# All 512 first-part tokens by row in a decoder trunk: 1024 row steps, 544 dense tokens, and more row steps with each product of the second part

## The chip, the core and the metric

The kernel runs on one core of a Trainium2 chip. The metric is device time in microseconds (us), the median of several executions. The profile shows one execution of the same program, with its engines: TensorE (PE, its weight loads shown apart as PEld), VectorE (DVE), ScalarE (ACT), GpSimd (POOL) and the queue engine SyncE (SP), and the 16 DMA engines.

## What is computed

One decoder layer for 1024 prompt tokens and 32 sample tokens, all in fp32, with model width 1024. The cut of the reference that matters here is the expert layer (PEER) at the end:

```
qh = x @ w_q                              # 8 heads x 256
v1, i1 = top_k(qh[..., :128] @ keys_1.T, 16);  v2, i2 = top_k(qh[..., 128:] @ keys_2.T, 16)
sc, ci = top_k(v1[:, None] + v2[None, :], 16)      # per token and head: 16 of 16384 experts
e, g   = expert numbers, softmax(sc)
hid    = gelu(einsum('thkd,td->thk', u_tab[e], x))
y      = einsum('thkd->td', (g * hid) * v_tab[e])
out    = LayerNorm2(ALPHA * h + y)
```

Before it stand the input product, a state-space scan with its convolution, a dilated window attention, the output product and LayerNorm1. So each token needs 128 rows of `u_tab` and 128 rows of `v_tab` (1024 floats each), picked by its own expert numbers.

## The kernel before

**Two parts.** The prompt is worked in two parts of 512 tokens (`PARTS`), the 32 sample tokens with the first. Each part runs `first` (queries, keys, values, attention, and the convolutions of B and C), `second` (twelve products for x with convolution and scan, then twelve for the gate z), `third` (the output product, 16 half products called `WO`, and LayerNorm1) and `route` (16 query products and the search for the experts). A product is `step`: a 1024x128 weight against all tokens of the part, in three passes (high x high, high x low, low x high), 24 or 48 matmuls. In the second part the split weights `whi` and `wlo` are read back from memory (`ws`), 2 x 512 KB for each product.

**Two ways through the expert layer.** After part one, its tokens' experts are known. For 448 of its 512 tokens (`TG`) the rows go one by one: generator `gathers` makes row steps. A row step is one indirect DMA on POOL (L1845) that fetches, for 128 tokens, one expert row each (128 x 4 KB, 512 KB), and one DVE operation over 128x1024: for `u` a product with the token and its sum (L1871), for `v` a scaled addition into the accumulator (L1876). A block of 128 tokens takes 128 u steps and 128 v steps; the last block has 64 tokens, laid as two halves over the 128 partitions, and takes 64 and 64. That is 896 steps. Six row buffers (`ROWS`) let row k+5 be fetched behind step k.

All other tokens, the second part's 512, the 32 samples and the last 64 of part one (`EXTRA`), 608 together (`TE`), go the dense way in `dense`: the hidden values of all 16384 experts for all tokens, 256 products of a 1024x128 weight with 48 matmuls each, 320 and 288 columns wide (`TPC`). For this, `gates` first builds a table of gates: for each four tokens DVE makes a one-hot pair `oo` (L1624), POOL weighs one half (L1626), PE multiplies (L1633), ACT stores (L1643). There are 152 such groups: 8 for the samples, 16 for the 64 extra tokens, 128 for the second part. The first six dense products (`EARLY` ticks) run beside this work. The other 250 follow, and each reads a 512 KB weight that ACT and POOL split into `whi` and `wlo` (L366, L367; one split in seven is DVE's), and pieces `g` of the gate table.

**What sets the order.** Code is issued in the order of ticks. A product has a few ticks, spread over its matmuls, and at each tick every open lane runs by its rate. `GATHER` gives the row steps for each product of the four stages of the second part, and the last entry the rate for each tick beside the table; afterwards `dense` spreads what is left evenly over its products. All engines take their instructions in that order, so a row step stands in the queues of POOL and DVE between the instructions of the product. `EARLY` gives 152 ticks in all. At the end, the last two products are cut in two pieces of tokens, and between them the kernel issues all that is left of the row lane.

## Time and profile before

| | us |
|---|---|
| median of 3 runs | 3749.65 (3748.82 to 3754.33) |
| the profiled execution | 3745.24 |
| its span in the trace | 3743.3 |

| engine | busy us | share |
|---|---|---|
| PE | 3461.4 | 92% |
| DVE | 2600.5 | 69% |
| POOL | 2231.0 | 60% |
| ACT | 1205.4 | 32% |

DMA moved 994.91 MB, 266 GB/s over the span. The shares are means over stages with different limits. Part one takes the trace up to some 870 us, the second part up to 1720, the table of gates from 1730 to 2020, and the dense products from there to the end. A busy PE counts pipelined matmuls and is not PE at its peak: the pace of PE is read from the starts of matmuls that follow each other.

### The profile page before, as it was taken

To read this page: it belongs to the slowest core of one execution; us is meant where nothing else is said; L and a number is where in the kernel's file an instruction comes from. 1 tells how busy PE (TensorE), PEld (TensorE's weight loads), DVE (VectorE), ACT (ScalarE), POOL (GpSimd) and SP (SyncE) were. 2 spreads that over 40 slices of the span, in tenths; PEclk is the share of its full clock that TensorE was granted. 3 is DMA by queue.
4 is the path that set the end of the run, shared out by engine and by line. 5 is a ranking of instruction groups with operands and counts; after the bars stand their busy time and mean duration, and the time that the engine had idled before them with its cause. 6 is when DMAs were issued, how large, how long until landed. Compare 5 with 4: busy or idle time off the path is not lost.

```text
span 3743.3 us, 61910 instructions
## 1 busy us (share of the span) xinstructions
PE 3461.4 (92%) x22691; PEld 3132.8 (84%) x22691; DVE 2600.5 (69%) x5394; ACT 1205.4 (32%) x2195; POOL 2231.0 (60%) x2138
## 2 busy tenths in 40 slices
PE   7999999989799888896778999999999999999998
PEld 6757778988567666675777999999999999999997
DVE  2325654379668987589998867677767667777775
ACT  3422224252343233123565222222232222223223
POOL 3303555333444676313887877777778777777774
PEclk9999899999899999997889999999999999999999
DMA  7565447996557669742557999999999999999994
GB/s 248 192 207 185 144 149 241 371 343 214 163 168 293 235 217 337 304 141 72 202 204 267 342 328 339 336 322 314 320 326 356 330 329 335 321 315 321 333 330 138
DMA packets 452624, 994.91 MB, mean 266 GB/s; under 512 B 47712, under 2 KB 158688, under 8 KB 449376
## 3 DMA queue, kind: packets, MB, share of 16 engines
q1 hardware_dynamic: 323296, 521.14, 41.1%
q0 software_dynamic: 129024, 469.82, 34.6%
q8 instruction: 179, 2.93, 0.3%
q14 instruction: 125, 1.02, 0.1%
HBM read 845.18 MB, written 174.34 MB: 272 GB/s over the span
## 4 chain that ended last, share of the span: by engine, by line
PE 53%; DVE 16%; DMA 5%; POOL 5%; issue 4%; ACT 2%; SPq 0%; POOLq 0%; DVEq 0%; ACTq 0%
PE P L447 42%; PE P L1767 5%; DVE oo L1624 2%; DMA wlo<-ws 2%; DVE cv L751 2%; DVE row L1871 1%; PE P L712 1%; POOL row L1845 1%; DVE mr L1363 1%; PE P L689 1%; POOL oo L1626 1%; DVE keys L1367 1%; DVE keys L1361 1%; PE P L1633 1%; POOL eq L1564 1%
## 5 line engine op out<-in xcount | busy, mean ns | idle before, releaser
L367 POOL TENSOR_TENSOR wlo<-wraw,whi 128x512 fp32r<-128x512 f32 x524 | 678.5, 1300 | 495.6 <-ACT whi L366 438.5
L366 ACT ACTIVATE whi<-wraw 128x512 fp32r<-128x512 f32 (+1 forms) x668 | 406.1, 625 | 1305.7 <-PE P L447 563.7
L447 PE MATMUL P<-hh,whi 128*128 128x320 f32 (+3 forms) x2648 | 656.2, 313 | 13.4 <-DMA whi<-ws 5.7
L447 PE MATMUL P<-hl,whi 128*128 128x320 f32 (+3 forms) x2648 | 653.4, 311 | 3.2 <-POOL hl L1318 2.9
L447 PE MATMUL P<-hh,wlo 128*128 128x320 f32 (+3 forms) x2648 | 647.4, 310 | 7.6 <-DMA wlo<-ws 3.9
L1876 DVE SCALAR_TENSOR_TENSOR P<-row,hid,P 128x1024 f32<-128x1024 f32 x448 | 575.8, 1285 | 40.3 <-DMA row<-in_v,ecol 23.9
L1871 DVE SCALAR_TENSOR_TENSOR row<-row,P 128x1024 f32<-128x1024 f32 x403 | 478.8, 1214 | 66.1 <-DMA row<-in_u,ecol 29.6
L1845 POOL DMA_INDIRECT row<-in_u,ecol x384 | 386.9, 1008 | 191.6 <-DVE row L1871 100.9
L447 PEld LDWEIGHTS P<-hh,whi 128*128 128x128 f32 x2648 | 445.5, 191 | 24.9 <-DMA whi<-ws 7.0
L447 PEld LDWEIGHTS P<-hh,wlo 128*128 128x128 f32 x2648 | 443.7, 190 | 17.7 <-DMA wlo<-ws 5.9
L447 PE MATMUL P<-xh,whi 128*128 128x272 f32 (+4 forms) x1288 | 431.2, 345 | 27.0 <-ACT xh L366 15.0
L447 PEld LDWEIGHTS P<-hl,whi 128*128 128x128 f32 x2648 | 444.9, 191 | 12.6 <-POOL hl L1318 4.2
L1845 POOL DMA_INDIRECT row<-in_v,ecol x384 | 375.9, 979 | 118.4 <-DVE P L1876 47.1
L447 PE MATMUL P<-xl,whi 128*128 128x272 f32 (+4 forms) x1288 | 418.8, 335 | 7.4 <-POOL xl L367 6.8
L447 PE MATMUL P<-xh,wlo 128*128 128x272 f32 (+4 forms) x1288 | 417.4, 334 | 3.2 <-DMA wlo<-ws 3.2
L447 PE MATMUL P<-ah,wlo 128*128 128x320 f32 (+1 forms) x1536 | 341.8, 302 | 3.6 <-POOL wlo L367 3.6
L447 PE MATMUL P<-ah,whi 128*128 128x320 f32 (+1 forms) x1536 | 342.8, 302 | 0.0
L447 PE MATMUL P<-al,whi 128*128 128x320 f32 (+1 forms) x1536 | 341.5, 301 | 0.0
L447 PEld LDWEIGHTS P<-xh,whi 128*128 128x128 f32 (+1 forms) x1288 | 246.6, 195 | 57.5 <-ACT xh L366 16.6
L367 DVE TENSOR_TENSOR wlo<-wraw,whi 128x512 fp32r<-128x512 f32 (+1 forms) x144 | 133.6, 928 | 229.8 <-ACT whi L366 210.4
L447 PEld LDWEIGHTS P<-xl,whi 128*128 128x128 f32 (+1 forms) x1288 | 246.5, 195 | 33.9 <-POOL xl L367 8.7
L447 PEld LDWEIGHTS P<-xh,wlo 128*128 128x128 f32 (+1 forms) x1288 | 245.8, 195 | 29.4 <-DMA wlo<-ws 5.0
(386 smaller groups left out, 6110.7 us busy)
## 6 DMA issues: line engine op xcount, KB each, us to landing
wraw<-in_ut SPq DMA_DIRECT2D x256, 256.0 KB, 5.4
wraw<-in_vd SPq DMA_DIRECT2D x256, 256.0 KB, 5.0
ws<-whi SPq DMA_DIRECT2D x152, 256.0 KB, 5.1
ws<-wlo SPq DMA_DIRECT2D x152, 256.0 KB, 5.0
whi<-ws SPq DMA_DIRECT2D x152, 256.0 KB, 5.2
wlo<-ws SPq DMA_DIRECT2D x152, 256.0 KB, 5.5
gd<-gst SPq DMA_DIRECT2D x19, 2048.0 KB, 7.5
g<-gd SPq DMA_DIRECT2D x90, 320.0 KB, 10.9
```

The lines of the kernel that those rows point to most:

```text
L366: nc.scalar.activation(hi, src, AF.Copy)
L367: (eng or nc.vector).tensor_tensor(lo, src, hi.bitcast(F32), op=ALU.subtract)
L447: nc.tensor.matmul(outs[i], w[a][:, k, :m], x[b][k][:, s:s + n], start=first and st, stop=last and sp)
L689: nc.tensor.matmul(sc[:, a:b], qz[:, hh, qt * 128:(qt + 1) * 128], kk[:, a:b], start=True, stop=True)
L712: nc.tensor.matmul(pv[row, :128], vv[:, k, row], pT[:, k, :], start=k == 0, stop=k == nt - 1)
L751: nc.vector.scalar_tensor_tensor(cv[:, 3:n], xr[:, k:k + m], cw[:, k:k + 1], cv[:, 3:n], op0=ALU.mult, op1=ALU.add)
L1361: nc.vector.max_index(idx[:, 0:8], vals[:, 0:8], src)
L1624: nc.vector.tensor_tensor(oo, iota.unsqueeze(1).unsqueeze(1).to_broadcast([128, 2, 4, 128]), eT[:, 0:2, t0:t0 + 4].unsqueeze(3).to_broadca ...
L1767: nc.tensor.matmul(outs[i][j], self.ws[q0 + i][wi][:, e, :], x[xi][e][:, s:s + m], start=e == p == 0, stop=e == last and p == 2)
L1845: nc.gpsimd.indirect_dma_start(out=rows[k], out_offset=None, in_=t["uv"[tab]], in_offset=bass.IndirectOffsetOnAxis(ap=tables(gi)[0][:, s:s ...
L1871: nc.vector.scalar_tensor_tensor(r, r, 1.0, at, op0=ALU.mult, op1=ALU.mult, accum_out=hid[:, s:s + 1])
L1876: nc.vector.scalar_tensor_tensor(at, r, hid[:, s:s + 1], at, op0=ALU.mult, op1=ALU.add)
```

## The change

The 64 tokens that went the dense way go by row: four whole blocks of 128 tokens, 1024 row steps. The dense tokens are then 544, so a dense product has matmuls of 288 and 256 columns, and the table has 136 groups. The half-filled block is gone with its copies, its halves' sum (`up`) and the 16 groups that stood between the samples and the second part's first block. `GATHER` gives more row steps for each product of the second part: 4 for 2.5, 4.2 for 3.2 and 3.5 for 3. A row fetch now waits, in the code, until its block is chosen. Most of the other lines turn constants into pairs, one for each part, with the values as before.

```diff
-EXTRA = 64
-TG = TD - EXTRA
-NX = EXTRA + NS
-TE = PD + NX
+TE = PD + NS
-GATHER = [2.5, 3.2, 3, 0.0, 0.2]
+GATHER, GATHERT = [[0, 0, 0, 0], [4, 4.2, 3.5, 0.0]], 0.2
...
     def pace(self, region):
-        self.rate = GATHER[region] / TICKS[self.hf][region]
+        self.rate = GATHER[self.hf][region] / TICKS[self.hf][region]
...
         if self.last:
-            others = [self.lane(self.experts(sp, *v)) for v in zip(((self.smp_e, self.smp_g), (self.ecol[-1], self.gate[-1])), (NS, 128), self.given)]
+            others = [self.lane(self.experts(sp, (self.smp_e, self.smp_g), NS, self.given))]
...
     def gates(self, sp):
-        work = [(NS, PD + EXTRA, 0), (EXTRA, PD, 128 - EXTRA)] + [(m, s, 0) for s, m in tiles]
-        given = 2
-        groups = [(w, t) for w in range(len(work)) for t in range(work[w][2], work[w][2] + work[w][0], 4)]
+        work = [(NS, PD)] + list((m, s) for s, m in tiles)
+        given = 1
+        groups = [(w, t) for w in range(len(work)) for t in range(0, work[w][0], 4)]
...
-            if t0 == work[w][2] and 0 < w < len(work) - 1:
+            if t0 == 0 and w < len(work) - 1:
                 gen = experts(w + 1)
             next(gen, 0)
-            if t0 == work[w][2] + work[w][0] - 4 * OBUFS:
+            if t0 == work[w][0] - 4 * OBUFS:
+                while w < given and self.top.live:
+                    yield
                 for _ in gen:
                     pass
...
     def gathers(self):
-        plan = [(gi, tab, s) for gi in range(NTG) for tab in range(2) for s in range(min(128, TG - gi * 128))]
+        plan = [(gi, tab, k) for gi in range(NTG) for tab in range(2) for k in range(128)]
...
-                    if m < 128:
-                        up = gp.tile([128, D], F32, name="up", tag="gh")
-                        nc.sync.dma_start(up[:m], acc[m:])
-                        nc.vector.tensor_tensor(acc[:m], acc[:m], up[:m], op=ALU.add)
-                    self.norm2(acc[:m], t["y"][gi * 128:gi * 128 + m], m)
+                    self.norm2(acc, t["y"][gi * 128:gi * 128 + 128], 128)
```

Counted in the order of the two programs on DVE: of the row steps, 167 stood ahead of the first table group, 30 among the groups and 699 behind them; now 226, 27 and 771. Of those ahead, 26 stood before the convolutions of B and C in the second part, 23 among these, 35 among the twelve products for x, and 83 in the gate products and `WO`; now 41, 37, 46 and 102. Part one's instructions keep their order.

The first place is DVE among the products for x in `second` (`cv` is the convolution, `E`, `hst`, `cbm`, `xd` belong to the scan). Before:

```order
L751 SCALAR_TENSOR_TENSOR cv<-xr,convw,cv 128x512 x3
L1871 SCALAR_TENSOR_TENSOR row,hid<-row,P 128x1024 x2
L756 SCALAR_TENSOR_TENSOR y<-xr,cv 128x512
L950 TENSOR_TENSOR E<-P,E 128x384
L951 TENSOR_TENSOR E<-E,P 128x384
L952 TENSOR_TENSOR hst<-hst,P 128x384
L955 SCALAR_TENSOR_TENSOR y<-y,chans,E 128x128 x3
L1871 SCALAR_TENSOR_TENSOR row,hid<-row,P 128x1024
L919 TENSOR_TENSOR cbm<-P,cst 128x128
```

and now:

```order
L749 SCALAR_TENSOR_TENSOR cv<-xr,convw,cv 128x512 x3
L1869 SCALAR_TENSOR_TENSOR row,hid<-row,P 128x1024 x2
L754 SCALAR_TENSOR_TENSOR y<-xr,cv 128x512
L1869 SCALAR_TENSOR_TENSOR row,hid<-row,P 128x1024
L948 TENSOR_TENSOR E<-P,E 128x384
L949 TENSOR_TENSOR E<-E,P 128x384
L950 TENSOR_TENSOR hst<-hst,P 128x384
L953 SCALAR_TENSOR_TENSOR y<-y,chans,E 128x128 x3
L1869 SCALAR_TENSOR_TENSOR row,hid<-row,P 128x1024
L917 TENSOR_TENSOR cbm<-P,cst 128x128
```

A fourth row step has come into the product, ahead of the scan's sums.

The second place is DVE near the start of the table, where the experts of the second part's first block are worked out (`eq` is compared on DVE, weighed on POOL, summed on DVE into `ef`). Before:

```order
L1562 TENSOR_TENSOR eq<-sf,cf 128x1024
L1624 TENSOR_TENSOR oo<-P,eT_14102 128x1024
L1876 SCALAR_TENSOR_TENSOR P<-row,hid,P 128x1024
L1624 TENSOR_TENSOR oo<-P,eT_14102 128x1024 x2
L1567 TENSOR_REDUCE ef<-eq 128x64
L1624 TENSOR_TENSOR oo<-P,eT_14102 128x1024
L1562 TENSOR_TENSOR eq<-sf,cf 128x1024
L1624 TENSOR_TENSOR oo<-P,eT_14102 128x1024 x2
```

and now:

```order
L1564 TENSOR_TENSOR eq<-sf,cf 128x1024
L1569 TENSOR_REDUCE ef<-eq 128x64
L1564 TENSOR_TENSOR eq<-sf,cf 128x1024
L1569 TENSOR_REDUCE ef<-eq 128x64
L1571 CAST ei<-ef 128x128
L1580 TENSOR_SCALAR ej<-ei 128x128
L1581 TENSOR_SCALAR ej<-ei 128x128
L1583 CAST en<-ej 128x256
```

The groups that stood between the comparing and the summing are gone, and DVE meets `ef` directly behind `eq`.

The third place is POOL among the dense products (row fetches and weight splits). Before:

```order
L367 TENSOR_TENSOR wlo<-wraw,whi 128x512 x2
L1845 DMA row<-in_v,ecol_76 128x1024 x3
L367 TENSOR_TENSOR wlo<-wraw,whi 128x512 x2
L1845 DMA row<-in_v,ecol_76 128x1024 x2
L367 TENSOR_TENSOR wlo<-wraw,whi 128x512
L1845 DMA row<-in_v,ecol_76 128x1024
L367 TENSOR_TENSOR wlo<-wraw,whi 128x512
L1845 DMA row<-in_v,ecol_76 128x1024 x3
L367 TENSOR_TENSOR wlo<-wraw,whi 128x512
L1845 DMA row<-in_v,ecol_76 128x1024 x2
```

and now:

```order
L365 TENSOR_TENSOR wlo<-wraw,whi 128x512 x2
L1843 DMA row<-in_v,ecol_77 128x1024 x3
L365 TENSOR_TENSOR wlo<-wraw,whi 128x512 x2
L1843 DMA row<-in_v,ecol_77 128x1024 x4
L365 TENSOR_TENSOR wlo<-wraw,whi 128x512
L1843 DMA row<-in_v,ecol_77 128x1024 x2
L365 TENSOR_TENSOR wlo<-wraw,whi 128x512
L1843 DMA row<-in_v,ecol_77 128x1024
L365 TENSOR_TENSOR wlo<-wraw,whi 128x512
L1843 DMA row<-in_v,ecol_77 128x1024 x2
```

Against seven splits there stood eleven fetches and now there stand twelve.

## Rows read from the trace of the kernel before

**Rows 1.** Windows by stage: length, busy us of five engines, clock, DMA share, GB/s.

```profile
980.00:1106.00 126.00, 122.55 (x685) 90.34 (x684) 85.60 (x185) 52.91 (x129) 71.60 (x52) 1.00 0.56 183
1106.00:1189.00 83.00, 80.13 (x409) 60.52 (x408) 59.21 (x119) 31.30 (x66) 33.07 (x37) 1.00 0.69 243
1189.00:1321.00 132.00, 113.32 (x573) 85.58 (x572) 125.19 (x194) 38.86 (x78) 85.12 (x96) 0.94 0.74 265
1321.00:1455.00 134.00, 114.51 (x582) 85.83 (x583) 106.90 (x191) 44.50 (x84) 99.98 (x97) 0.96 0.75 262
1455.00:1570.00 115.00, 97.84 (x458) 77.69 (x458) 73.78 (x70) 13.52 (x19) 58.64 (x56) 0.94 0.94 354
1730.00:2020.00 290.00, 222.04 (x1510) 205.27 (x1510) 276.04 (x391) 173.44 (x177) 230.10 (x214) 0.88 0.54 198
2200.00:2300.00 100.00, 100.00 (x718) 100.00 (x717) 70.33 (x113) 28.06 (x47) 77.77 (x72) 1.00 0.97 350
2800.00:2900.00 100.00, 100.00 (x719) 100.00 (x718) 75.95 (x119) 27.97 (x47) 80.92 (x76) 1.00 1.00 359
```

**Rows 2.** Timeline of PE, dense products: start, length, group of two matmuls (320, 288).

```profile
2499.75 0.44 PE L447 MATMUL P<-al,whi 128*128 128x320 f32 x2
...
2501.70 0.44 PE L447 MATMUL P<-ah,wlo 128*128 128x320 f32 x2
```

**Rows 3.** Timeline of PE in part one, matmuls of 272 columns.

```profile
204.78 0.29 PE L447 MATMUL P<-xh,whi 128*128 128x272 f32 x1
...
206.17 0.29 PE L447 MATMUL P<-xh,wlo 128*128 128x272 f32 x1
```

**Rows 4.** Timeline of POOL, dense products: row fetches and weight splits.

```profile
2304.03 0.96 POOL L1845 DMA_INDIRECT row<-in_u,ecol  x1
2305.29 0.94 POOL L1845 DMA_INDIRECT row<-in_u,ecol  x1 [0.30 <-issue]
2306.24 1.30 POOL L367 TENSOR_TENSOR wlo<-wraw,whi 128x512 fp32r<-128x512 f32 x1
2307.70 0.96 POOL L1845 DMA_INDIRECT row<-in_u,ecol  x1 [0.16 <-issue]
```

**Rows 5.** Waits of POOL, 2100 to 3650 us: total, times, longest.

```profile
POOL wlo L367 <- ACT whi L366: 163.6, 184, 5.8
...
POOL row L1845 <- DVE row L1871: 26.1, 73, 1.8
POOL row L1845 <- DVE P L1876: 24.7, 40, 1.7
```

**Rows 6.** DMA queues and issues, 2100 to 3650 us; the issues' last number is us to landing.

```profile
DMA packets 232784, 508.31 MB, mean 328 GB/s; under 512 B 19890, under 2 KB 88017, under 8 KB 232648
...
row<-in_v,ecol POOLq DMA_INDIRECT x283, 6.4
row<-in_u,ecol POOLq DMA_INDIRECT x256, 6.8
```

**Rows 7.** The same view in `WO`, 1470 to 1540 us; GB/s in 40 slices of it.

```profile
GB/s 392 397 227 267 252 296 224 303 352 417 418 404 406 400 401 404 393 408 391 404 401 397 398 404 398 401 403 403 405 401 399 404 399 400 401 411 387 393 407 401
...
whi<-ws SPq DMA_DIRECT2D x20, 256.0 KB, 13.5
...
row<-in_v,ecol POOLq DMA_INDIRECT x33, 10.1
```

**Rows 8.** Groups by line on DVE, 980 to 1470 us: count, busy us, mean ns, idle before.

```profile
L1871 DVE SCALAR_TENSOR_TENSOR row<-row,P 128x1024 f32<-128x1024 f32 x83 | 98.7, 1212 | 2.7 <-DMA row<-in_u,ecol 2.7
...
L1871 DVE SCALAR_TENSOR_TENSOR row<-row,gh 128x1024 f32<-128x1024 f32 x45 | 64.8, 1452 | 0.0
```

**Rows 9.** The same view of 1730 to 2020 us, DVE and POOL.

```profile
L1624 DVE TENSOR_TENSOR oo<-P,eT 128x1024 f32<-128x1024 f32 x152 | 178.2, 1215 | 6.3 <-ACT eT L1587 2.8 <-PE P L1585 2.1 <-PE P L1633 1.3
...
L1564 POOL TENSOR_TENSOR eq<-eq,cf 128x1024 f32<-128x1024 f32 x8 | 18.9, 2367 | 0.0
```

**Rows 10.** Timeline of DVE, end of the first block's experts in the table.

```profile
1795.71 2.36 DVE L1624 TENSOR_TENSOR oo<-P,eT 128x1024 f32<-128x1024 f32 x2 [1.59 <-ACT eT L1587]
```

**Rows 11.** Groups by line on DVE, 2100 to 3650 us.

```profile
L1876 DVE SCALAR_TENSOR_TENSOR P<-row,hid,P 128x1024 f32<-128x1024 f32 x337 | 433.2, 1285 | 20.0 <-DMA row<-in_v,ecol 10.5 <-DMA row<-in_v,halfe 2.4 <-ACT P L1849 1.3
L1871 DVE SCALAR_TENSOR_TENSOR row<-row,P 128x1024 f32<-128x1024 f32 x320 | 380.1, 1215 | 63.4 <-DMA row<-in_u,ecol 26.8 <-issue 25.6 <-DMA row<-in_u,halfe 8.0
```

**Rows 12.** The chain that ended last, its end: start, length, what.

```profile
3681.92 1.03 ACT acc L1849
3682.97 3.61 DMA up<-acc
3686.67 1.23 DVE acc L1882
...
3698.10 13.46 PE P L447 x92
```

More of the change, by code (lines that the diff above doesn't have):

```diff
@@ L200 @@
 OUTS = {
-    "y": (TG, D),
+    "y": (TD, D),
     "y1": (128, 8, TE),
@@ L1271, in third @@
                 norms[i].run()
-            self.step(self.x, [out[i] if np_ == 2 else out[0][:, s:s + n]], [(s, n)], 4, q=q0, ahead=i == 0)
+            self.step(self.x, [out[i] if np_ == 2 else out[0][:, s:s + n]], [(s, n)], TICKS[hf][3], q=q0, ahead=i == 0)
         self.close(f"z{hf}", f"y{hf}", f"att{hf}", f"x{hf}")
@@ L1850, in seat @@
             return dst
-        for k in range(LOOK):
-            fetch(k)
+        fetch(LOOK - 1)
         for k, (gi, tab, s) in enumerate(plan):
-            m = min(128, TG - gi * 128)
+            while ahead[0] <= k:
+                fetch(k)
+                yield
             hs = heads[gi]
```

155 lines of the change are left out of this document (77 added, 78 removed).

## The prediction

> **What bounds the kernel now.** I first read the windows by stage, to see which engine has no idle time in which stage, then the starts in PE's timeline for its true pace, then the queues of POOL, DVE and DMA for how far behind PE they are. Among the dense products (2020 us to the end) PE is busy 100% at granted clock 1.00, its 2.4 GHz level, with 718 matmuls in 100 us [rows 1]. Seven pairs of matmuls, 320 and 288 columns, start within 2501.70 - 2499.75 = 1.95 us [rows 2], 278.6 ns a pair, so a product of 24 pairs takes 6.69 us. There PE is the bound, but three others are close. The windows give the DMA share as 0.97 and 1.00 and DVE as 70 and 76% [rows 1]. POOL looks like 78 to 81% [rows 1], but between two fetches it loses 0.30 us, and 0.16 us behind a split [rows 4], so its true load is higher. In the second part's stages PE is not alone: DVE is 95% busy in the products for x (125.2 of 132 us), and DMA has share 0.94 in `WO` [rows 1]. In the table stage DVE is busy 276.0 of 290 us [rows 1].
>
> **Part one** keeps its order on every engine; I count nothing for it.
>
> **The second part, 59 more row steps (226 for 167).** A step costs DVE 1.45 us while the token rows lie in SBUF, 1.21 us afterwards [rows 8]. By stage, with the counts of the order:
> - Attention, 15 more: 15 x 1.45 = 22 us of DVE. DVE is busy 86 of 126 us, DMA 0.56 [rows 1], so there is room, and PE (busy 123) sets the pace. A step ahead of a softmax delays it by 1.45 us now and then. I take 5 us, between 0 and 22.
> - Convolutions of B and C, 14 more: 17 us of DVE and 14 x 0.524 MB. In 83 us DVE idles 24 and DMA runs at 0.69 [rows 1]. About half fits: 10, between 0 and 17.
> - Products for x, 11 more: 13 us on a DVE that idles 7 of 132 us [rows 1]. I take 12, between 6 and 13.
> - Gate products, some 12 more: 15 us of DVE at 80% and 15 of POOL at 75% [rows 1]; 6, between 0 and 15.
> - `WO`, some 7 more: 7 x 0.524 MB = 3.7 MB. DMA holds 400 GB/s here for most of 70 us [rows 7], so the bytes take 9 us, and nothing else hides them. I take 9.
>
> Sum 42 us. With every step at full price it would be 59 x 1.21 = 71, with everything that idle time can hold hidden 15.
>
> **The table stage** loses 16 groups of 1.215 us on DVE [rows 9]: -19 us, as DVE is its bound. It loses the cover of the first block's experts with them. DVE now waits twice for POOL's 2.37 us over `eq` [rows 9], since `ef` stands right behind it, and once for the transposes ahead of the next group, 1.6 us already now [rows 10]. That is 7 us, and 12 us remain as a gain (0 to 19: if POOL has a queue of its own when `eq` comes, the whole gain goes). The 16 freed ticks hold only the rest of a product.
>
> **The dense products** are the largest term. PE: part one has matmuls of 272 columns, two of them 544 as after the change, and eleven of them start within 206.17 - 204.78 = 1.39 us [rows 3], 126.4 ns each. A product then needs 48 x 126.4 ns = 6.07 us, 0.62 less than now. If PE stayed the bound, 246 products (the 250 less the first and last few) would give 246 x 0.62 = 153 us. What can follow at that pace?
> - Row steps. There were 658 fetches in 1550 us (283 + 256 [rows 6], and 119 of the half block), or 2.84 for each 6.69 us. The rest of the order grew from 699 to 771, so it is 3.13 for each product.
> - POOL. From fetch to fetch 1.26 us (2304.03 to 2305.29), fetch to split 0.95, split to fetch 1.46 [rows 4]. So a fetch costs 1.26 and a split 1.15. A product has two splits, of which POOL does six in seven, 1.7: now 2.84 x 1.26 + 1.7 x 1.15 = 5.53 us, then 5.90. That is 97% of 6.07, in a queue that takes its work in order. Today POOL also waits 163.6 us for ACT and 51 us for DVE in 232 products [rows 5], 0.93 us for each. Nearly all of this would have to go.
> - DMA. 508.31 MB in 1550 us [rows 6] is 2.19 MB for a product. Then: rows 3.13 x 0.524 = 1.64, weights 0.52, gate table 0.14 (128 x 8 x 544 values of 4 bytes for 16 products), together 2.30 MB. At 6.07 us this asks 379 GB/s. `WO` held 400 [rows 7], so it needs 5.75 us at least; the busiest 100 us of the dense stage held 359 [rows 1], and by that it is 6.41 us.
> - DVE: a v step takes 1.285, a u step 1.215 us [rows 11]. The 0.29 more steps are 0.36 us, and the operations over 544 columns instead of 608 give 0.1 back; 85% of 6.07 us. Not the bound.
>
> So PE lets go, and POOL and DMA, each at 95% or more, take over together. I take 6.30 us a product: POOL's 5.90 and 0.4 of its 0.93 us of waits, which also lies between DMA's two bounds. Gain 246 x 0.39 = 96 us, between 0 and 153.
>
> **The end.** Rows and weights share POOL's queue, so the split for PE's last piece stands behind the last row block, and PE starts that piece at 3698.1 us only [rows 12]. The half block's folding, 3.61 us of DMA and 1.23 of DVE, is on that chain [rows 12] and goes. The last piece and the norm, 45 us, have a tenth fewer columns: together -9 (-4 to -9).
>
> **The sum**, against the profiled execution of 3745.2 us: 42 - 12 - 96 - 9 = -75, so 3670. That execution lies 4.4 us under the median of the runs, which I add: **3675 us**, 2.0% faster.
>
> **The rivals.**
> 1. *PE keeps the bound*, 6.07 us a product. For it: weights are split two products ahead and rows are fetched five steps ahead, so a wait on POOL need not reach PE. Against it: POOL at 97%. 42 - 12 - 153 - 9 = -132: 3618 us.
> 2. *A ceiling of DMA at 359 GB/s.* For it: no 100 us of the dense stage did more, and the small pieces of the gate table are in its mix. Against it: 400 GB/s in `WO` with the same 4 KB rows. 6.41 us a product, gain 69: 42 - 12 - 69 - 9 = -48: 3702 us. The Trainium skill, "DMA: Bandwidth & Descriptors", section Specifications, gives a limit of about 358 GB/s from HBM for one core; by it the product takes 2.30 / 0.358 = 6.42 us. The dense stage's best window agrees (359), the 400 of `WO` does not, so I give it the smaller chance.
> 3. *The row loop, slower than before.* Fetch k+5 needs the buffer that step k-1 frees, so six steps take at least one landing, one DVE step (1.29) and the split that stands ahead on POOL (1.30). The period at 6.07 us is 6 x 6.07 / 3.13 = 11.6 us, so it decides from a landing of 9.0 us on. Landing now takes 6.4 to 6.8 us [rows 6], but 10.1 where DMA was saturated, with 13.5 for weights beside it [rows 7]. With 10.1 the product takes 3.13 x 12.7 / 6 = 6.62 us, a gain of 17 us only. Late rows then also hold DVE's queue in the second part, behind which the scan waits, so its steps cost their full 71: 71 - 12 - 17 - 9 = +33: 3783 us.
>
> That the order does not change as the text says is excluded: the counts show 59 and 72 more steps in the two places.
>
> **How the numbers follow.** The forecast gets 0.43, rival 1 gets 0.18, rival 2 gets 0.15, rival 3 gets 0.24. The range goes from 3618, rival 1's own time, to 3772, some two thirds of the way from 3750 to rival 3's time; it leaves out the part of rival 3 that pays all prices in full (0.12) and what goes beyond rival 1 (0.08). A measurement of this kernel can tell some 0.2% from no change, 7.5 us. The forecast, rival 1 and two thirds of rival 2 lie below that (the rest of rival 2, with a second part near its 71, comes to within it): 0.43 + 0.18 + 0.10 = 0.71 faster. Within it 0.05 of rival 2 and 0.03 of rival 3, 0.08; slower 0.21.
>
> **What would show it.** Right: in the dense stage PE no longer 100% busy but some 96%, 48 matmuls in 6.2 to 6.4 us, POOL's waits for ACT well under 0.7 us a product, DMA at 360 to 370 GB/s with share 1.00; the x products longer by about 1 us each, `WO` by 9 us; the table stage 12 us shorter with two DVE waits for POOL's `eq`. Wrong: PE at 100% (rival 1); a flat 359 GB/s with PE and DVE waiting for DMA (rival 2); DVE waiting for rows in every product and landings of 9 us or more (rival 3); or a second part that grows by much more than 71 us, for which no row here gives a reason.

## The result, and the profile after

The change takes the kernel from 3750.8 us (median of 4 runs, 3748.8 to 3754.3) to **3713.6 us** (4 runs, 3710.4 to 3716.2), a ratio of 0.9909 with a 95% interval of 0.9894 to 0.9924. That is 37 us, half of the 75 us that the sum promised. The time lies in the range of 3618 to 3772.

Three events stand in every trace and cut it into stages: the first search step of part one's route (`mr<-keys` on VectorE), the last copy of a query (`qh`, at the end of the second part's route) and the last store of the gate table (`gd<-gst`). With them, in us:

| | before | after | difference | predicted |
|---|---|---|---|---|
| up to the first search step (part one) | 790.7 | 788.5 | -2 | 0 |
| from there to the last query (second part) | 927.8 | 991.5 | **+64** | +42 |
| to the last store (table stage) | 300.6 | 276.7 | **-24** | -12 |
| to the end (dense stage) | 1724.2 | 1653.2 | **-71** | -105 |

The rows of these events, in the views of the tiles `mr`, `qh` and `gd<-gst`, before and then after (behind the count: shortest, median and longest in ns, then first and last start in us):

```profile
L1363 DVE MATCH_REPLACE8 mr<-keys,sc x128: 271/276/284, 790.7 to 1735.1; 128x128 f32<-128x128 f32 x128
...
L473 ACT ACTIVATE qh<-P x48: 371/395/602, 786.8 to 1718.6; 128x272 f32<-128x272 f32 x32, 128x512 f32<-128x512 f32 x16
...
L1645 SPq DMA_DIRECT2D gd<-gst x19: 319/320/383, 1760.4 to 2019.1; - x19
```

```profile
L1362 DVE MATCH_REPLACE8 mr<-keys,sc x128: 265/275/287, 788.5 to 1797.7; 128x128 f32<-128x128 f32 x128
...
L471 ACT ACTIVATE qh<-P x48: 370/396/602, 782.4 to 1779.9; 128x272 f32<-128x272 f32 x32, 128x512 f32<-128x512 f32 x16
...
L1647 SPq DMA_DIRECT2D gd<-gst x17: 319/320/423, 1845.5 to 2056.7; - x17
```

Windows of the changed kernel, the second part's stages first, then table stage and four windows of the dense stage. Columns as in [rows 1]; x counts instructions:

```profile
980.00:1106.00 126.00, 118.37 (x659) 88.16 (x657) 98.22 (x191) 49.08 (x120) 84.30 (x61) 0.99 0.67 215
1106.00:1204.00 98.00, 83.67 (x423) 61.93 (x422) 75.09 (x154) 33.47 (x72) 50.37 (x49) 0.95 0.83 294
1204.00:1360.00 156.00, 125.22 (x577) 94.29 (x575) 146.51 (x227) 38.95 (x78) 100.09 (x113) 0.87 0.75 272
1360.00:1511.00 151.00, 121.77 (x585) 89.34 (x586) 125.81 (x167) 49.63 (x90) 113.47 (x110) 0.92 0.80 280
1511.00:1590.00 79.00, 69.29 (x262) 52.23 (x261) 59.57 (x51) 8.61 (x12) 49.18 (x48) 0.91 1.01 381
1791.80:2056.60 264.80, 188.24 (x1364) 176.80 (x1365) 246.02 (x368) 154.42 (x159) 207.61 (x193) 0.87 0.54 194
2200.00:2300.00 100.00, 97.23 (x770) 96.69 (x769) 80.82 (x130) 28.11 (x48) 84.20 (x78) 1.00 1.01 369
2600.00:2700.00 100.00, 90.22 (x686) 88.95 (x686) 70.49 (x113) 27.17 (x44) 77.14 (x69) 0.97 0.95 342
2800.00:2900.00 100.00, 97.97 (x777) 97.11 (x776) 81.39 (x116) 28.39 (x49) 84.40 (x79) 1.00 1.01 368
3100.00:3200.00 100.00, 81.41 (x616) 80.48 (x615) 64.19 (x89) 24.40 (x39) 72.53 (x65) 0.91 0.92 330
```

Two things are to be seen. In the second part the same work takes longer windows: for the x products 577 matmuls in 156 us, where before 573 took 132 [rows 1]. In the dense stage the clean windows hold 770 to 777 matmuls where before held 718 [rows 1]: 48 of them take 6.23 us, a little better than the 6.30 that I took. The 13 windows of 100 us from 2100 to 3600 us without a row block's end hold 767 on average, 6.26 us a product. But the two with an end, shown above, hold 686 and 616, some 11 and 20 us short at that pace.

What the engines wait for in the dense stage, 2100 to 3500 us (total, times, longest), has changed sides. ACT, which splits the weights, waited most for PE before; now it waits for weights to land, and VectorE for rows. POOL's wait for ACT has gone from 147.5 to 41.3 us over these 1400 us. Before, then after:

```profile
ACT whi L366 <- PE P L447: 358.8, 72, 5.7
...
POOL wlo L367 <- ACT whi L366: 147.5, 160, 5.8
...
ACT whi L366 <- DMA wraw<-in_ut: 84.1, 26, 11.8
ACT whi L366 <- DMA wraw<-in_vd: 75.7, 21, 9.5
...
DVE row L1871 <- DMA row<-in_u,ecol: 26.8, 33, 3.1
```

```profile
...
ACT whi L364 <- DMA wraw<-in_vd: 321.6, 116, 8.5
ACT whi L364 <- DMA wraw<-in_ut: 260.5, 93, 8.9
DVE row L1869 <- DMA row<-in_u,ecol: 110.1, 120, 3.6
...
DVE P L1874 <- DMA row<-in_v,ecol: 69.3, 78, 3.0
POOL wlo L365 <- ACT whi L364: 41.3, 33, 4.4
```

POOL's timeline shows what lies in the window of 616 matmuls. The last norm of a row block multiplies and adds its gain and bias (`lng`) on POOL, and the two transfers are issued only then; POOL waits 8.89 us for them, works 4.78, and fetches no row and splits no weight for 14 us:

```profile
3126.03 0.94 POOL L1843 DMA_INDIRECT row<-in_u,ecol  x1 [0.31 <-issue]
3135.86 4.78 POOL L1895 TENSOR_TENSOR acc<-acc,lng 128x1024 f32<-128x1024 f32 x2 [8.89 <-DMA lng<-in_ln]
3140.78 0.98 POOL L1843 DMA_INDIRECT row<-in_u,ecol  x1
```

VectorE's timeline has the echo of it, a row step that comes 7.51 us late:

```profile
3146.11 1.22 DVE L1869 SCALAR_TENSOR_TENSOR row<-row,P 128x1024 f32<-128x1024 f32 x1 [7.51 <-POOL wlo L365]
```

### The profile page after: what moved, and what is told of

The parts are those of the page before. It is cut to its first block, busy times and chain, and to the rows that moved or that the text cites. A ratio compares the mean times of both kernels' runs of the same rounds, so it can differ in the third digit from the quotient of the medians.

```text
span 3709.9 us, 62089 instructions
## 1 busy us (share of the span) xinstructions
PE 3311.5 (89%) x22560; PEld 2973.0 (80%) x22560; DVE 2717.9 (73%) x5565; ACT 1177.8 (32%) x2178; POOL 2346.7 (63%) x2250
## 5 line engine op out<-in xcount | busy, mean ns | idle before, releaser
L1874 DVE SCALAR_TENSOR_TENSOR P<-row,hid,P 128x1024 f32<-128x1024 f32 x512 | 657.9, 1285 | 123.0 <-DMA row<-in_v,ecol 111.2
L445 PE MATMUL P<-hh,whi 128*128 128x288 f32 (+3 forms) x2648 | 630.8, 303 | 32.8 <-DVE al L1703 16.0
L1843 POOL DMA_INDIRECT row<-in_u,ecol x512 | 520.4, 1016 | 217.2 <-DVE row L1869 89.7
L1869 DVE SCALAR_TENSOR_TENSOR row<-row,P 128x1024 f32<-128x1024 f32 x440 | 527.0, 1215 | 152.8 <-DMA row<-in_u,ecol 132.2
L445 PE MATMUL P<-hl,whi 128*128 128x288 f32 (+3 forms) x2648 | 626.0, 301 | 2.8 <-POOL hl L1317 2.5
L445 PE MATMUL P<-hh,wlo 128*128 128x288 f32 (+3 forms) x2648 | 621.3, 300 | 5.9 <-DMA wlo<-ws 5.0
L1843 POOL DMA_INDIRECT row<-in_v,ecol x512 | 498.7, 974 | 173.6 <-DVE P L1874 69.6
L445 PE MATMUL P<-ah,whi 128*128 128x288 f32 (+1 forms) x1536 | 327.5, 293 | 23.7 <-DVE r L1721 23.7
L445 PE MATMUL P<-ah,wlo 128*128 128x288 f32 (+1 forms) x1536 | 326.2, 292 | 18.0 <-POOL wlo L365 18.0
L445 PE MATMUL P<-al,whi 128*128 128x288 f32 (+1 forms) x1536 | 324.8, 291 | 0.0
```

Source lines behind the costliest of these rows:

```text
L445: nc.tensor.matmul(outs[i], w[a][:, k, :m], x[b][k][:, s:s + n], start=first and st, stop=last and sp)
L1843: nc.gpsimd.indirect_dma_start(out=rows[k0], out_offset=None, in_=t["uv"[tab]], in_offset=bass.IndirectOffsetOnAxis(ap=self.ecol[gi][:, s: ...
L1869: nc.vector.scalar_tensor_tensor(r, r, 1.0, at, op0=ALU.mult, op1=ALU.mult, accum_out=hid[:, s:s + 1])
L1874: nc.vector.scalar_tensor_tensor(at, r, hid[:, s:s + 1], at, op0=ALU.mult, op1=ALU.add)
```

## The experiments

Their stages, in us of each profiled execution, and the medians of the timed runs:

| run | second part | table | dense | median | against before |
|---|---|---|---|---|---|
| e_after | 990.2 | 277.1 | 1651.4 | 3712.2 | 0.9911 |
| e_oldpace | 931.6 | 276.7 | 1738.6 | 3723.9 | 0.9945 |
| e_before_newpace | 994.2 | 312.1 | 1717.6 | 3815.4 | 1.0177 |
| e_halfdve | 966.3 | 270.4 | 1636.0 | 3662.8 (one run) | - |
| e_halfboth | 935.1 | 271.5 | 1586.7 | 3587.0 (one run) | - |
| e_lnkeep | 993.9 | 277.1 | 1641.6 | 3707.2 | 0.9903 |
| e_lnearly | 990.8 | 277.0 | 1649.9 | 3712.1 | 0.9908 |
| e_lndve (again: e_lndve_b) | 990.3 (992.9) | 277.1 (277.0) | 1630.2 (1633.0) | 3692.2 (3694.0) | 0.9850 (0.9851) |
| e_more | 1048.1 | 279.0 | 1567.9 | 3686.9 | 0.9840 |
| e_more2 | 991.5 | 294.9 | 1621.6 | 3700.8 | 0.9882 |
| e_gflat | 994.6 | 276.7 | 1599.6 | 3657.5 | 0.9760 |
| e_after_g | 993.5 | 282.8 | 1615.6 | 3676.9 | 0.9814 |
| e_before_g | 931.2 | 300.6 | 1725.9 | 3744.9 | 0.9994 |
| e_best (again: e_best_b) | 993.1 (994.1) | 280.0 (280.1) | 1595.5 (1593.1) | 3657.7 (3657.8) | 0.9763 (0.9766) |
| e_best_old | 958.7 | 280.2 | 1641.3 | 3668.1 | 0.9789 |
| e_best2 | 996.5 | 280.1 | 1588.8 | 3648.1 | 0.9731 |

The 95% intervals of the ratios reach 0.0009 to 0.0024 to either side, 3 to 9 us. Three runs are bases only:

> The changed kernel once more, beside the three variants of this group, as their base: 0.991 of the time before, some 3714 us. Nothing is told apart by it alone.

> The kernel whose last norm is finished on VectorE from SBUF, once more, as the base of this group: 0.985 of the time before, some 3692 us.

> The kernel with the new layout of the gate table and the last norm on VectorE once more, as the base of the run beside it: 0.976 of before, some 3658 us.

**The two halves of the change, each alone.** The tokens by row with the old pace, and the new pace without the tokens:

```diff
-GATHER, GATHERT = [[0, 0, 0, 0], [4, 4.2, 3.5, 0.0]], 0.2
+GATHER, GATHERT = [[0, 0, 0, 0], [2.5, 3.2, 3, 0.0]], 0.2
```

> The changed kernel with the old numbers of row steps in the second part (2.5, 3.2 and 3 for each product instead of 4, 4.2 and 3.5); the 64 tokens still go by row. Some 59 row steps move from the second part back into the dense stage. Theory A (in the dense stage the transfers are the bound, at the 368 GB/s that its windows show): 59 rows of 0.524 MB are 31 MB, 84 us more there; the second part gives back the 64 us that it grew by; the whole is some 20 us longer than the changed kernel, about 3734 us. Theory B (GpSimd's queue is the bound, 1.26 us a fetch): 59 x 1.26 = 74 us more, 10 us longer, about 3724. Theory C (TensorE still bounds the dense stage, only the ends of the row blocks cost something): the dense stage stays and the whole is 64 us shorter, about 3650.

```diff
-GATHER = [2.5, 3.2, 3, 0.0, 0.2]
+GATHER = [4, 4.2, 3.5, 0.0, 0.2]
```

> The kernel before (64 tokens still dense, 608 columns) with the new numbers of row steps for each product of the second part: 59 steps more there, 59 fewer in the dense stage. Theory A (the two halves of the change only pay together: TensorE bounds the dense stage of before at 6.69 us whatever the rows do): the second part 55 to 64 us longer, the dense stage within 10 us, 3795 to 3810 us, a ratio of 1.013 to 1.017. Theory B (the rows already cost the dense stage of before something): 59 x 0.5 us or more come back there, 3780 us or less.

The second part of the first of them is back at 931.6 us. The kernel before took 927.8 us there, and 931.2 with another layout of the gate table (e_before_g, below), so the 64 tokens alone cost it nothing that shows, and the 59 row steps cost 59 us (990.2 - 931.6), 0.99 us each. In the kernel before they cost 63 to 66 (994.2 less 931.2 or 927.8). The dense stage of the first pays 87 us for 59 rows, 1.48 us each, near theory A's 84; its runs, though, spread from 3717 to 3741 us, and their median of 3724 alone would fit theory B. In the kernel before, the 59 steps give the dense stage 7 us: theory A, PE was the bound there. The table stage of that run is 12 us longer, which I had not foreseen: the first row block now ends inside it (its gain and bias are asked for at 2071.5 us, and the last store of the table is at 2095.5). So the pace alone loses 66 us, the tokens alone gain 21, and the two together 37 (32 beside the runs of this group): the tokens make the room in the dense stage, the pace fills it.

**What a row step costs, VectorE or bytes.** The first run halves VectorE's step, the second the bytes too. Each leaves out half of every row's product or sum, and the second finds its half rows at other places of the two tables:

```diff
-nc.vector.scalar_tensor_tensor(r, r, 1.0, at, op0=ALU.mult, op1=ALU.mult, accum_out=hid[:, s:s + 1])
+nc.vector.scalar_tensor_tensor(r[:, :512], r[:, :512], 1.0, at[:, :512], op0=ALU.mult, op1=ALU.mult, accum_out=hid[:, s:s + 1])
...
-nc.vector.scalar_tensor_tensor(at, r, hid[:, s:s + 1], at, op0=ALU.mult, op1=ALU.add)
+nc.vector.scalar_tensor_tensor(at[:, :512], r[:, :512], hid[:, s:s + 1], at[:, :512], op0=ALU.mult, op1=ALU.add)
```

> The changed kernel, VectorE's row steps on 512 of the 1024 columns (the other half of each row's product and sum is left out); the transfers are as before. Second part, theory A (a row step costs its time on VectorE): 226 steps at some 0.65 instead of 1.29 us, the 991 us from the end of part one to the end of the route fall to 880 to 930. Theory B (its transfers, or rows that land late, are the price): they stay within 10 us of 991. Dense stage, theory A (DMA bound): its 1651 us stay within 10. Theory C (VectorE has come near the bound there): it falls by 20 us or more.

```diff
-nc.gpsimd.indirect_dma_start(out=rows[k0], out_offset=None, in_=t["uv"[tab]],
+nc.gpsimd.indirect_dma_start(out=rows[k0][:, :512], out_offset=None, in_=t["uv"[tab]].rearrange("n (a d) -> (n a) d", a=2),
```

> As the run with half of VectorE's row step, and only these 512 columns are fetched (2 KB instead of 4 KB a row; half of the rows' product is left out). To be compared with that run: only the bytes differ, GpSimd issues as many fetches. Dense stage, theory A (DMA bound at some 368 GB/s): a product needs 1.5 MB instead of 2.3, TensorE becomes the bound at 6.07 us, about 385 to 400 matmuls in 50 us everywhere, DMA share under 0.75; 40 us shorter at the steady pace and 10 to 25 more at the block ends, where the norm's gains land sooner. Theory B (GpSimd's queue bound, 5.90 us and its waits): the steady pace stays within 1% and the stage within 15 us. Second part: within 10 us of the run with half of VectorE's step if its transfers cost nothing there; shorter by 15 us or more if they do (in the products of WO and of B and C above all).

In the second part half of VectorE's step gives 24 us (990.2 to 966.3), half of the bytes another 31 (to 935.1). Neither theory is right alone: both are a price there, about equally. Where each is paid is read between events of the second part that stand in every trace: the first search step, the last `bc<-xr,cv` (the convolutions of B and C), the first and the last `z<-P` (the gate products), the first and the last `qh`. In us:

| run | attention, B and C | x products | gate products | `WO` and norm | queries |
|---|---|---|---|---|---|
| before | 402.7 | 140.6 | 116.1 | 151.5 | 117.0 |
| after | 424.0 | 160.9 | 130.1 | 160.9 | 115.6 |
| e_after | 425.3 | 159.5 | 131.2 | 159.1 | 115.2 |
| e_oldpace | 404.9 | 143.6 | 115.8 | 152.1 | 115.3 |
| e_halfdve | 414.2 | 150.8 | 127.6 | 158.1 | 115.7 |
| e_halfboth | 409.2 | 142.5 | 124.7 | 143.5 | 115.2 |
| e_lndve_b | 426.1 | 161.0 | 130.7 | 159.7 | 115.5 |
| e_more | 457.0 | 168.6 | 133.8 | 174.3 | 114.5 |
| e_more2 | 456.7 | 147.9 | 116.5 | 154.9 | 115.6 |

Against e_after, half of VectorE's step gives 11, 9, 4 and 1 us in the first four stretches, and half of the bytes another 5, 8, 3 and 15. So in `WO` the bytes are the price, and in the two stretches ahead of the gate products it is both. In the gate products, where the 59 steps cost 15 us (131.2 - 115.8), neither gives much; POOL's fetches, which both runs keep, are a candidate that no run tries.

The dense stage falls by 15 us with half of VectorE's step, between the 10 and the 20 of the two theories, and by 49 more with half of the bytes. Its windows of the first run, then two of the second:

```profile
2150.00:2550.00 400.00, 389.67 (x3064) 387.81 (x3063) 229.91 (x403) 114.57 (x196) 335.43 (x313) 0.99 1.01 372
```

```profile
2100.00:2500.00 400.00, 400.00 (x3185) 399.99 (x3184) 231.94 (x420) 119.09 (x203) 349.79 (x322) 1.00 0.80 247
...
2550.00:2900.00 350.00, 348.80 (x2783) 348.36 (x2782) 201.76 (x400) 103.94 (x176) 305.51 (x282) 1.00 0.80 249
```

With the full bytes VectorE is busy 57% and the pace is as it was (e_after has 3045 matmuls there), 3064 matmuls in 400 us, at a DMA share of 1.01. With half of the bytes PE is busy 100%, 3185 in 400 us, 6.03 us a product, though POOL issues as many fetches and is busy 87%. So DMA bounds the dense stage of the changed kernel, and POOL does not.

**The ends of the row blocks.** Gain and bias loaded once; then loaded early for each block; then loaded once and applied by VectorE:

```diff
 dp = self.open("dn", 2)
+self.lng = dp.tile([128, 2, D], F32, name="lng", bufs=1)
+nc.sync.dma_start(self.lng, t["ln2"].unsqueeze(0).to_broadcast([128, 2, D]))
```

> The changed kernel, with the gain and bias of the last norm loaded once, when the dense stage opens, into 8 KB of their own; from the second row block on GpSimd finds them there and does not wait for two transfers of 0.52 MB. Theory A (the 10 and 19 us that TensorE loses about 2630 and 3130 us come from GpSimd waiting 8 to 11 us in its queue for these transfers, with the row fetches and weight splits behind it): 20 to 30 us shorter, 3684 to 3694 us, and the two windows come back from 686 and 616 matmuls to some 760. Theory B (they come from GpSimd's two operations of 2.4 us and VectorE's norm themselves): at most 6 us shorter, from the 2.1 MB that are no longer moved, 3708 us or more.

```diff
+if tab == 1 and s == 96 and self.lng is not None:
+    self.lngs = [self.lng.tile([128, D], F32, name=f"lng{i}", bufs=1) for i in range(2)]
+    for i in range(2):
+        nc.sync.dma_start(self.lngs[i], t["ln2"][i:i + 1, :].to_broadcast([128, D]))
```

> As the run that keeps the gain and bias, but they are loaded for each row block as before, 32 row steps ahead of their use, into buffers of their own: the same bytes as the changed kernel, without the wait. Theory A (the wait): as short as the run that keeps them, but for 2.1 MB at 368 GB/s, some 6 us: 3690 to 3700 us. Theory A' (the bytes of these transfers cost the time, not the wait): as the changed kernel, 3714 us. Theory B: as the changed kernel.

```diff
-nc.gpsimd.tensor_tensor(acc, acc, gb[:m], op=op)
+(nc.gpsimd if self.lng is None else nc.vector).tensor_tensor(acc, acc, gb[:m], op=op)
```

> As the run that keeps the last norm's gain and bias in SBUF, and from the second row block on VectorE applies them instead of GpSimd (two operations on 128 x 1024, some 1.2 us each by the row steps' duration). GpSimd then has nothing of a block's end in its queue. Theory A (the ends cost time because GpSimd fetches no rows for 10 to 14 us there, and the transfers, which bound this stage, run dry meanwhile): the DMA share of 2600 to 2650 and 3100 to 3150 us rises from 0.90 and 0.84 to at least 0.97, the windows lose less than a third of what they lost, and the time falls by another 10 to 15 us against the run that keeps them: 3692 to 3697 us. Theory B (the ends cost time for DVE's norm and the late rows ahead of it): no change against that run, 3707 us.

My first theory does not hold as it stands. Without the wait, but with the same bytes, nothing is gained in all (3712.1 beside 3712.2): the two windows come back in part, to 706 and 675 matmuls, and the rest of the stage loses as much. With 2.1 MB less, 5 us, which is no more than the interval and about what the bytes cost. With nothing of the norm on POOL the gain is 20 us (3712.2 to 3692.2, and 3694.0 the second time). So it is not the transfers alone that cost the time, it is the stop of POOL's queue as a whole: with `lng` loaded once POOL still waited 14.0 us for VectorE's norm, in three places, and worked 4.8 us in each. What share the wait has and what share the work is not separated. The two windows with VectorE's version:

```profile
2600.00:2700.00 100.00, 93.89 (x730) 93.44 (x729) 79.68 (x125) 31.25 (x51) 79.26 (x74) 0.97 1.00 358
3100.00:3200.00 100.00, 90.71 (x701) 90.52 (x701) 81.56 (x117) 30.51 (x49) 79.88 (x73) 0.95 0.98 359
```

The DMA share is up from 0.95 and 0.92 to 1.00 and 0.98, the matmuls from 686 and 616 to 730 and 701. A little under half of the loss against 767 stays, where theory A allowed a third, and the 50 us from 3100 reach a share of 0.93, not 0.97; what holds them is not tried. While POOL stands still no rows are asked for, and what DMA, the bound of this stage, does not move then is lost.

**Where to put the rows.** On that kernel, more of them in attention and B and C; and the same number, moved there from the later stages:

```diff
-[4, 4.2, 3.5, 0.0]]
+[6, 4.2, 3.5, 0.0]]
...
-[4, 4.2, 3.5, 0.0]]
+[6, 3.2, 3, 0.0]]
```

> As the base, with 6 row steps instead of 4 for each product of attention and of the convolutions of B and C: 263 row steps ahead of the gate table instead of 226, 37 fewer in the dense stage. Theory A (the dense stage pays 1.4 us a row in transfers as long as they bound it; attention and B and C pay 0.7 us a row, as the 29 steps more did there with 20 us): second part 26 us longer, dense stage 40 us shorter (its floor is TensorE), some 14 us less than the base: 3678 us. Theory B (with more of them the steps cost VectorE's full 1.29 us there as well): second part 48 us longer, the whole as the base or longer, 3692 to 3700 us.

> As the base, with 6, 3.2 and 3 row steps for each product of the three stretches instead of 4, 4.2 and 3.5: 231 row steps ahead of the gate table instead of 226, some 37 more in attention and B and C and some 32 fewer in the products for x, the gate products and WO. Theory A (a step costs 0.7 us in attention and B and C but 1.3 to 1.5 us in the later stages): 37 x 0.7 = 26 us more there, 32 x 1.35 = 43 us less behind: second part 17 us shorter, dense stage 5 us shorter, 3670 to 3676 us. Theory B (one price everywhere): second part within 8 us, the whole 3685 to 3695 us.

In the first the second part is 55 us longer (1048.1 - 992.9), past theory B's 48, but in the table of stretches above only 31 of them lie in attention and B and C, where the 37 steps were added: 0.8 us each, near theory A's 0.7. The other 24 lie behind, 15 of them in `WO` and norm, where the first row block now ends (its gain and bias are asked for at 1645.4 us). The dense stage, which has that end no longer, gave back 65, more than A's 40, and 7 us remain, about the size of the intervals. The second costs 31 us in attention and B and C and gives 32 behind: 0.8 and 1.0 us a step, nearer to one price than to theory A's two. It is slower by 7 us; the first row block ends inside the table stage (its gain and bias are asked for at 2040.6 us), and that stage is 18 us longer.

**Why DMA stops at 371 GB/s.** The dense stage reads the gate table in pieces of 512 bytes, 17 for each partition. First a run that reads it in long stretches from another place, then the layout changed so that the right values lie in long stretches:

```diff
-nc.sync.dma_start(gs[c, i][:, rows], self.gd[rows, :, e0:e0 + 4, :].rearrange("b j i t -> j b i t"))
+nc.sync.dma_start(gs[c, i][:, rows].rearrange("j b i t -> j (b i t)"), self.gd[e0 // 4 % b].rearrange("j i t -> j (i t)")[:, :m])
```

> As the base, but the dense stage reads its gate weights as whole stretches of 2 KB or more for each partition, from another place of the table (so it weighs with the wrong gates), instead of pieces of 512 bytes: the same bytes in fewer, longer pieces. Theory A (the pieces keep the transfers at 367 GB/s in this stage, where WO held 400): the rate rises to 380 GB/s or more where it is the bound, the dense stage is 20 to 30 us shorter, 3665 to 3672 us. Theory B (the pieces cost nothing that matters, 6 of 100 bytes): within 6 us of the base.

```diff
-self.gd = dpool.tile([TE // 32, 128, NE, 32], F32, name="gd")
+self.gd = dpool.tile([NE // 4, 128, TE // 32, 4, 32], F32, name="gd")
-nc.sync.dma_start(gs[c, i][:, rows], self.gd[rows, :, e0:e0 + 4, :].rearrange("b j i t -> j b i t"))
+nc.sync.dma_start(gs[c, i][:, rows], self.gd[e0 // 4][:, rows])
```

> The changed kernel, with the gate table laid out in DRAM so that the dense stage reads it as whole stretches of 2 KB or more for each partition (the pieces of 512 bytes are then on the writing side, in the table stage); the result is that of the changed kernel. Theory A (the short pieces lower what the transfers reach in the dense stage, which they bound): dense stage 25 to 33 us shorter, as in the run that read other places; table stage within 5 us, since its DMA share is 0.54: 3680 to 3690 us. Theory B (the gain of that run came from the other place it read, not from the pieces): within 6 us of 3713. Theory C (the pieces only move their price to the writing side): dense stage shorter, table stage longer by as much.

> The kernel before with the same layout of the gate table. Theory A (TensorE bounds the dense stage of before, so cheaper transfers give nothing): within 6 us of before. Theory B (the transfers already cost it something at 328 GB/s): 10 us shorter or more.

The first two were as theory A had it, and more. The DMA view of 2150 to 2550 us, first of the base (e_lndve_b), then with long stretches (e_gflat): as many bytes in 52,545 packets instead of 65,508.

```profile
DMA packets 65508, 148.55 MB, mean 371 GB/s; under 512 B 5790, under 2 KB 23310, under 8 KB 65470
```

```profile
DMA packets 52545, 149.92 MB, mean 375 GB/s; under 512 B 5829, under 2 KB 5829, under 8 KB 52507
```

In the changed kernel the layout gives 35 us (3712.2 to 3676.9; the stage 36). Two windows, first without it (e_after), at 371 and 370 GB/s, then with it (e_after_g), at 379 and 381:

```profile
2700.00:3050.00 350.00, 337.86 (x2653) 335.50 (x2652) 284.70 (x362) 97.02 (x166) 295.33 (x273) 0.99 1.01 371
3200.00:3550.00 350.00, 343.47 (x2709) 342.00 (x2708) 283.16 (x382) 100.74 (x175) 295.77 (x273) 1.00 1.01 370
```

```profile
2700.00:3050.00 350.00, 342.60 (x2713) 341.37 (x2712) 286.90 (x370) 100.11 (x172) 301.12 (x280) 1.00 1.01 379
3200.00:3550.00 350.00, 348.83 (x2774) 348.22 (x2774) 294.02 (x379) 101.61 (x174) 304.00 (x281) 1.00 1.01 381
```

From 2150 to 2550 us it gives nothing, 370 GB/s and 3045 matmuls in both; and the two windows with a block's end rise more than the others, from 694 and 615 to 716 and 698 matmuls. In the kernel before the same edit gives nothing (0.9994, 0.9985 to 1.0003), since PE is the bound; a window of it:

```profile
2700.00:3050.00 350.00, 350.00 (x2510) 350.00 (x2509) 246.57 (x362) 96.05 (x159) 264.41 (x242) 1.00 0.92 333
```

The writing side pays 6 us in the table stage (277.1 to 282.8). How much of the 35 us is the rate alone is not separated: 371 to 380 GB/s would be 2.4%, some 38 us over the stage, if all of it were bound by transfers. That the length of the pieces counts and not their place rests on two runs that read different places and gain about the same.

**Together.** The new layout and VectorE's last norm; with fewer rows in the second part; and with gain and bias loaded at the opening of the table stage, so that the first block finds them too:

> The changed kernel with the new layout of the gate table and with the last norm finished on VectorE from gains in SBUF. If the two add up (20 us and 30 us): 3660 to 3665 us, 0.976 of before. If TensorE takes the bound over on the way: 3665 to 3675 us.

> As that, with 3.2, 3.6 and 3 row steps for each product of the second part: 190 row steps ahead of the gate table instead of 226. Theory A (with cheaper transfers the dense stage is near TensorE's pace, so that 36 more rows cost it less than the 1.0 to 1.5 us that each costs the second part): second part 38 us shorter, dense stage 25 us longer, some 3648 us. Theory B (transfers still bind at 380 GB/s, 1.38 us a row): the two cancel, within 8 us of the run before it.

> As the base, but the gain and bias of the last norm are loaded when the table stage opens instead of when it ends, so that the first row block, which ends between the table stage and the dense products, finds them in SBUF and finishes on VectorE too. Theory A (the first 750 matmuls of the dense stage take 116 to 124 us, where the pace gives 98 and the start itself some 10, because GpSimd waits 11.8 us for these transfers there): 8 to 12 us shorter, 3646 to 3650 us. Theory B (the start is long for the first weights, rows and gate table, which all come at once): within 4 us of the base.

The two causes add up: 3657.7 us, 0.976 of before. With 36 rows fewer in the second part it is 10 us slower: the second part gains 34, the dense stage loses 46, 1.27 us for each row, though its first block's end comes late enough to be finished on VectorE. So PE is not the only bound there yet, which fits transfers that still bind, and the 59 steps were not moved too far. POOL's wait at the first block's end, in the base of the last run (2050 to 2120 us):

```profile
POOL acc L1900 <- DMA lng<-in_ln: 12.0, 1, 12.0
```

It is gone in the last one, which takes 3648.1 us, 10 less than its base, as theory A expected, with intervals of some 6 us on both. (Its profiled execution was the longest of its five, 3659.9 us, so the table shows only 4 us of that.) The 40 us from about 3 us behind the last store of the table hold 210 matmuls instead of 151, base first:

```profile
2066.00:2106.00 40.00, 25.67 (x151) 24.00 (x152) 20.72 (x28) 12.54 (x20) 21.49 (x16) 0.79 0.79 283
```

```profile
2073.00:2113.00 40.00, 33.38 (x210) 31.90 (x211) 29.78 (x40) 13.68 (x22) 22.11 (x19) 0.83 0.75 265
```

At 0.9731 of before (0.9717 to 0.9746) it is the fastest kernel here that gives the whole result. A late window of it is bound by PE again, 2781 matmuls in 350 us, 6.04 us a product, beside a DMA at its end as well:

```profile
3200.00:3550.00 350.00, 349.20 (x2781) 349.01 (x2780) 286.20 (x364) 97.36 (x167) 301.25 (x279) 1.00 1.01 383
```

## Why the prediction was wrong by half

The direction was right, and PE did let go of the dense stage; three terms were mis-sized and one was missing.

- **Part one, 0.** Right (-2).
- **The second part, +42, measured +64.** The first failed step is the cover: I let idle time hide about half of what the steps ahead of `WO` ask of VectorE, 33 of 67 us left. By the table of stretches the kernel takes 21 us more in attention and B and C (5 + 10 forecast), 20 in the x products (12), 14 in the gate products (6), and 9 in `WO` (9), where I had counted the bytes as not hidden. The steps cost 0.99 us each. Ahead of `WO` I priced them on VectorE, at 1.21 us and more, and let idle time hide it; the halved runs show that bytes are a price there too, 5 and 8 us beside VectorE's 11 and 9 for half of each. For the gate products they show no price that is large enough, and the cause of those 14 us stays open. In the x products there are two smaller misses besides. The counts there (VectorE's groups of 1204 to 1360 us, line, count, busy us and mean ns) show 51 + 5 steps where before had 41 in its window, 15 more and not the 11 of the order; and each u step has a readout that I had left out:

```profile
L1869 DVE SCALAR_TENSOR_TENSOR row<-row,P 128x1024 f32<-128x1024 f32 x51 | 60.6, 1214 | 3.5 <-DMA row<-in_u,ecol 3.4
...
L1869 DVE DVE_READ_ACCUMULATOR row<-row,P 128x1 f32 x50 | 4.0, 81 | 0.0
```

  15 x 1.295 = 19 us of the 24 by which that window is longer than before's. My upper bound of 71 held; the value inside it did not.
- **The table stage, -12, measured -24.** The 16 groups gave their 20 us (136 instead of 152 `oo`), and the lost cover cost 5.6 us more of idle VectorE where I said 7, with the two waits for POOL's `eq`, 2.5 us each. Two things were not in the sum: 3 row steps fewer (3.9 us), and 5.7 us that VectorE's remaining operations took less. Groups of VectorE, 1791.8 to 2056.6 us:

```profile
L1626 DVE TENSOR_TENSOR oo<-P,eT 128x1024 f32<-128x1024 f32 x136 | 158.4, 1213 | 4.4 <-ACT eT L1589 2.9 <-PE P L1587 1.4
...
L1569 DVE TENSOR_REDUCE ef<-eq 128x64 f32<-128x1024 f32 x8 | 9.8, 1220 | 11.3 <-POOL eq L1566 11.2
...
L1583 DVE CAST en<-ej 128x256 f32<-128x256 int32 x4 | 1.1, 282 | 0.0
```

  That last cast took 865 ns in the kernel before, one of the four 2.62 us, and `eq` 1656 ns instead of now 1218. One went the other way, the first cast of `ci`, 1358 ns for 218. Read from the traces; no run tried it.
- **The dense products, -96, and the end, -9, measured -71 together.** The pace was right, 6.23 us in clean windows against 6.30 forecast, with the signs I had named: PE at 97 to 98%, 368 to 369 GB/s at a share of 1.01, POOL's waits for ACT down to 0.18 us a product. The reason was half right: DMA alone bounds it, and POOL's 5.90 us do not, since PE ran at 6.03 us with the same fetches. The missing term is the ends of the row blocks. I read the row loop and its landings, and did not ask what else stands in POOL's queue every 256 rows. The transfers of `lng` did stand in the trace of the kernel before: POOL waited for them at three block ends, 7.4, 6.8 and 12.3 us. But while PE was the bound, such a stop cost PE 5 us at the most; of the windows with these ends one held all of its 718 matmuls, and the other two these:

```profile
2100.00:2200.00 100.00, 97.70 (x689) 97.45 (x688) 68.65 (x77) 29.25 (x48) 72.58 (x65) 0.98 0.88 308
...
3300.00:3400.00 100.00, 96.28 (x681) 96.04 (x680) 66.90 (x70) 26.58 (x43) 66.25 (x60) 0.99 0.87 291
```

  With DMA at its end it costs more: taking the norm off POOL gave 20 us at the later ends and, with the long pieces, 10 at the first, of the 53 us that POOL waits or works at the four ends.

  The end, -9, did not come. I took the chain that ended last [rows 12] for time that PE loses. The waits of PE's weight loads from 3600 us on, before and then after, show that PE waited only 1.6 us for the last split, so that the half block's folding had little to give:

```profile
PEld P L447 <- POOL wlo L367: 1.6, 1, 1.6
```

```profile
PEld P L445 <- POOL wlo L365: 4.0, 1, 4.0
```

  From the start of PE's last piece to the end it is 43.7 us (3709.9 - 3666.2), where before it was 45.2 (3743.3 - 3698.1).

  Counted in matmuls (12,056 after the table in the changed kernel, at 767 in 100 us instead of 718), the pace alone is worth -108 us. Of this the start of the stage takes back some 13 us (from the last store of the table on, 150 matmuls in 43.3 us, where before 238 stood in 43.9), the two ends that lie in the windows 21 (30 us lost where before lost 9), and the time from 3600 us on 1 or 2. That estimate makes some -73 us, beside the -71 measured.

Of the rivals, rival 1 did not come, but the halved bytes produce its pace. Rival 2, a flat ceiling at 359 GB/s, is refuted as a number (369, and 383 with long pieces) and right in kind. Its 3702 us are the nearest to the measured time, by a compensation: its slower pace stood for the ends that neither it nor the forecast had. Of the signs of rival 3 one came in part: VectorE waited for rows 198 times in the 1400 us shown above, some 225 products, but for 0.9 us on average. The other did not: rows landed in 7.0 to 7.1 us, under the 9.0 from which it decides, and half of VectorE's step, which would have shortened that loop, left the pace as it was.

## What to carry to other kernels

When a change takes an engine off the bound, look in every queue that is next in line for what happens seldom: the end of a block, a norm, a load of constants. Slack had made it cheap, and it can now cost most of its length. A step that two resources carry is hidden only where both are idle at the same time; if the cover is read from one of them, take the full price as the likely value and not as the bound. And a transfer's bytes are not its cost: once DMA is the bound, look at the length of the pieces, which cost the kernel before nothing. Last, a chain that ends last is worth only what its end lets another engine do earlier: read that engine's wait first.
